# Recurrent mixer of a two-block network: when the chunk scores, the block transposes and the triangular solve stand in the program

## The chip, the cores and the metric

The kernel runs on one core of a Trainium2 chip. The metric is device time in microseconds (us) of one launch, from the core's clock. Before the change it is 1166.73 us, the median of 3 runs (1165.8 to 1170.56). Lower is better.

## The reference, cut to what matters

Two transformer blocks run on one sequence of 256 tokens and 1024 channels, all in float32. The change lies in the second layer of the first block, a recurrent time mix (WKV). Cut to what is touched:

```python
xr, xw, xk, xv, xa, xg = [h + xx * mu[i] for i in range(6)]   # xx: the token before, minus h
r, k, v = xr @ w_r, xk @ w_k, xv @ w_v
g = sigmoid(xg @ g1) @ g2
kk = heads(k * k_k); kk = kk / norm(kk)                        # 16 heads of 64
k = k * (1 + (a - 1) * k_a)
# per token t and head:
sa = state @ (-kk_t)
state = state * w_t + outer(sa, kk_t * a_t) + outer(v_t, k_t)
y_t = state @ r_t
y = groupnorm(y) * ln_w + ln_b + sum(r * k * r_k) * v
h = h + (y * g) @ w_o
```

## The kernel before, in words

The recurrence is not run token by token. The 256 tokens are cut into 4 chunks of 64. Within a chunk the dependence of each token's `sa` on the earlier tokens is a unit triangular system, and it is solved by blocks of 32 tokens. 16 heads x 4 chunks x 2 blocks give 128 systems of 32 x 32, one in each partition.

The function `rwkv` writes the stage in this order; the names are those that the profile prints for tiles.

- `k`: the keys' product in two halves (`key_half`), heads 0 to 7 and heads 8 to 15. Weights of `k`, `v` and `g` are used whole in float32, so each such product is two rows of the trace. While a half runs, `between0` or `between1` is called after each quarter.
- `keys(j)`, for a quarter j of the heads: VectorE and ScalarE build `AR` and `BK`, the scaled keys and queries. `squares(j)` multiplies the squares (`sqk`) with a pattern and gathers norms in `ssps`; `rkk(j)` forms the products for the bonus (`rk`).
- `scores(c, g)`: for chunk c and half g of the heads, 8 products on TensorE (`sce`, `sco`; 16 rows of the trace), then two masked copies on VectorE into `SC`.
- `norms()`: VectorE takes `ss` from `ssps`, and 16 small copies on SyncE's queue bring it into `pd`, one partition for each system. VectorE inverts `pd` to `ip`.
- `by_problems(g, bs)`: TensorE transposes the scores into `rb`, and copies bring them into `Ab`, one half of the tile `ABX`. The other half, `Xb`, starts with zeros and the inverses on its diagonal.
- `solve(s)`, s = 0 to 30: forward substitution on VectorE, small operations `tb<-ABX` and `ABX<-ABX,tb`, each waiting for the one before it.
- `values(0)`, `values(1)`: the product `v` in two halves, 8 steps of two instructions each, written as a generator (`next(v0)`, `next(v1)`), as are the gates (`g`, 4 steps). `by_tokens`: transposes of `BK` (`bkt`). `gate_turn`: transposes of the gate (`gt`, then `gz`, `gh`, `gl` on VectorE and ScalarE).
- Behind the solve: `xt` and `x` (X1) transpose its result, `q` and a second `x<-SC,X` form the block that couples the two halves of a chunk, `coefs` (`cf`) sums the bonus, `busy` are 8 products that fill time. Then `WY`, `U` and `S` run the chunks.

Weights come by DMA on SyncE's queue, 512 KB a chunk (`raw`), in the order in which the program takes them, into 4 buffers; where they are split, ScalarE makes `hi` and VectorE or GpSimd `lo`. PSUM has 8 banks (`bank`), shared by all of these.

The order of instructions on each engine is not exactly that of the code: the framework's scheduler orders them when the program is built, by the order written and by its own estimate of when operands and buffers are ready. Each engine then runs its own list in order. `L355`, `L358`, `L340`, `L343` and `L352` are the helpers `mm`, `tr`, `tt`, `stt` and `act`, so operations are told apart by their tiles.

Of the kernel before, what the change touches and what calls it, by code (L numbers as in the profile page):

```python
# [18 lines left out]
P = 128  # L19
T = 256  # L20
D = 1024
KD = 8
# [112 lines left out]
def full(name, layer, k, c0):  # L135
    return (name, layer, k * P, P, 0, ((c0, P),))
# [126 lines left out]
class Kern:  # L263
# [485 lines left out]
    def rwkv(self, sums, nxt):  # L749
        nc = self.nc  # L750
        h = self.h
        sp = self.sp
        ws = self.ws
# [39 lines left out]
        def mix(i, k, out):  # L793
            self.stt(out, xx[:, k, :], self.pv(f"mu{i}", k), hn[:, k, :], ALU.mult, ALU.add)
# [60 lines left out]
        for k in range(KD):  # L855
# [11 lines left out]
            if 3 <= k < 7:  # L867
                i, j = (k - 3) // 2, 2 * ((k - 3) % 2)
# [30 lines left out]
        def keys(j):  # L899

            ms, ps = two(j), psk[j]
            u, kku = self.mid("u", (P, 2, T)), self.mid("kku", (P, 2, T))
            for m in range(2):
                self.act(kku[:, m, :], half(ps, m), AF.Copy, scale=self.pv("k_k", 2 * j + m))
            for m in range(2):
                self.act(u[:, m, :], av(ms)[:, m, :], AF.Identity, scale=ka[:, 2 * j + m:2 * j + m + 1],
                         bias=ika[:, 2 * j + m:2 * j + m + 1])
            sq = self.mid("sqk", (P, 2, T))
            self.act(flat(sq), flat(kku), AF.Square)
            self.stt(arv(AR, j, 0), c4(kku), -1.0, dd(ms)[:, :, :, 0:64], ALU.mult, ALU.mult)  # L910
            t, kp = self.mid("t", (P, 2, T)), self.mid("kp", (P, 2, T))
            self.stt(t, av(ms), 1.0, kku, ALU.add, ALU.mult)
            self.tt(arv(BK, j, 0), c4(t), c4(di(ms)), ALU.mult)
            self.tt(flat(kp), ps, flat(u), ALU.mult)
            self.tt(arv(BK, j, 1), c4(kp), c4(di(ms)), ALU.mult)
            kps[j] = kp
            return sq

        def squares(j, sq):
            if not ssps:  # L920
                ssps.append(self.bank("ssps"))
            for m in range(2):
                mm = 2 * j + m
                self.mm(ssps[0][0:16, 0:T], self.cst("hind", 128)[:, mm * 16:(mm + 1) * 16], sq[:, m, :], mm == 0, mm == 7)
# [13 lines left out]
        def rkk(j):  # L938

            o = flat(rk[:, two(j), :])  # L940
            self.tt(o, o, flat(kps.pop(j)), ALU.mult)


        def key_half(g, between):
            pss = [self.bank("k") for _ in range(2)]
            for kk in range(4):
                w = ws.take_whole([full("rwkv_w_k", 0, k, m * P) for k in (2 * kk, 2 * kk + 1) for m in range(4 * g, 4 * g + 4)])
                for i, k in enumerate((2 * kk, 2 * kk + 1)):
                    for m in range(4):
                        self.mm(half(pss[m // 2], m), w[4 * i + m], xk[:, k, :], k == 0 and m % 2 == 0, k == KD - 1)  # L950
                between(kk)
            psk[2 * g], psk[2 * g + 1] = pss
# [5 lines left out]


        xv, xg = [self.xp.tile([P, KD, T], F32, tag=t, name=n) for t, n in (("xh", "xv"), ("xl", "xg"))]  # L960
        key_half(0, between0)
        sqs = {}

        def between1(kk):
            if kk < 2:
                sqs[kk] = keys(kk)
            else:
                squares(kk - 2, sqs[kk - 2])
                rkk(kk - 2)
            for k in (2 * kk, 2 * kk + 1):  # L970
                mix(5, k, xg[:, k, :])

        key_half(1, between1)


        psv = [[None, None] for _ in range(2)]

        def values(n):
            for tt in range(2):
                psv[tt][n] = self.bank("v")  # L980
            for k in range(KD):
                if k % 2 == 0:
                    ws.take_whole([full("rwkv_w_v", 0, q, (4 * n + i) * P) for q in (k, k + 1) for i in range(4)])
                    wt = ws.whole_chunk
                for tt in range(2):
                    self.mm(psv[tt][n], xv[:, k, tt * P:(tt + 1) * P], wt[:, 512 * (k % 2):512 * (k % 2) + 512], k == 0, k == KD - 1)
                yield


        SC = [pair("SC")[:, 0:4096].rearrange("p (i x t) -> p i x t", i=32, x=2) for _ in range(2)]  # L990
        tri = self.cst("tri", 128)
# [22 lines left out]
        def by_problems(g, bs):  # L1014
            for b in bs:
                p0 = 64 * b + 32 * g
                for e in range(2):
                    ps = self.bank("rb")
                    for i in range(16):
                        self.tr(ps[0:32, i * 32:(i + 1) * 32], SC[g][32 * b:32 * b + 32, :, 0, 32 * b + 16 * e + i],  # L1020
                                32, 32 * b)
                    o = Ab[p0:p0 + 32, 16 * e:16 * e + 16, :].rearrange("p a b -> p (a b)")
                    if e == 0:
                        nc.vector.tensor_copy(out=o, in_=ps[0:32, :])
                    else:
                        self.act(o, ps[0:32, :], AF.Copy)


        ip = self.tiny("ip", [P, 32], tag="pd")
        ABX = self.slot("ABX", (P, 2, 32, 32))  # L1030
        Ab, Xb = ABX[:, 0], ABX[:, 1]

        cf = self.tiny("cf", [P, 2, 16], tag="cf", bufs=3)
        cfps = []
# [16 lines left out]
        def solve(s):  # L1051
# [8 lines left out]
            for a, b in h:  # L1060
                o = Xb[:, s + 1 + a:s + 1 + b, 0:w]
                self.tt(o, o, tv[:, a:b, :], ALU.add)


        def gates():
            psg = self.bank("g")
            seg = [((0, P),), ((P, 32), (None, 96))]
            for k in range(KD):
                if k % 4 == 0:
                    ws.take_whole([("rwkv_g1", 0, q * P, P, 0, seg[i]) for q in range(k, k + 4) for i in range(2)])  # L1070
                    wt = ws.whole_chunk
                for tt in range(2):
                    self.mm(psg[:, tt * 160:tt * 160 + 160], xg[:, k, tt * P:(tt + 1) * P],
                            wt[:, 2 * P * (k % 4):2 * P * (k % 4) + 160], k == 0 and tt == 0, k == KD - 1)
                if k % 2:
                    yield psg

        v0, v1, ga = values(0), values(1), gates()
        next(v0)
        for j in (2, 3):  # L1080
            sqs[j] = keys(j)
        for _ in range(2):
            next(v0)
        for j in (2, 3):
            squares(j, sqs[j])
        norms()
        next(v0)
        for c in range(4):
            scores(c, 0)
            next(v0)  # L1090
        for c in range(4):
            scores(c, 1)
            psg = next(ga)
        next(v0, None)
        nc.vector.memset(Xb, 0.0)
        nc.vector.reciprocal(out=ip, in_=pd)
        nc.vector.tensor_copy(out=Xb.rearrange("p a b -> p (a b)")[:, 0:1024:33], in_=ip)
        for j in (2, 3):
            rkk(j)
        for g in range(2):  # L1100
            for b in range(2):
                by_problems(g, (b,))
        self.tt(Ab, Ab, ip.unsqueeze(2).to_broadcast([P, 32, 32]), ALU.mult)

        gm = self.mid("gm")
        gmt = gm[:, 0:448].rearrange("p (t c) -> p t c", t=2)
# [20 lines left out]
            q, o = slice(32, 64), slice(T, 2 * T)  # L1127
            self.tt(gh[q, o], z[q, o], gh[q, o].bitcast(F32), ALU.subtract)

        for s in range(14):  # L1130
            solve(s)
        for g in range(2):
            next(v1)
            by_tokens(g, (0, 1))
            next(v1)
            by_tokens(g, (2, 3))
        gate_turn()
        for s in range(14, 31):
            solve(s)
        for _ in range(4):  # L1140
            next(v1)
        self.dump("Xb", ABX)


# [12 lines left out]
        for b in range(2):  # L1157
            for e in range(4):
# [1 line left out]
                for i in range(8):  # L1160
                    self.tr(ps[0:32, i * 64:(i + 1) * 64], Xb[64 * b:64 * b + 64, 8 * e + i, :], 64, 64 * b)
                turned(lambda g: SC[g][32 * b:32 * b + 32, :, 0, 32 * b + 8 * e:32 * b + 8 * e + 8], ps)
        coefs(0)
        X1 = self.xp.tile([64, 2, 32, 32], F32, tag="xl", name="X1")
        for e in range(4):
            ps = self.bank("x1")
            for i in range(8):
                self.tr(ps[0:32, i * 64:(i + 1) * 64], Xb[0:64, :, 8 * e + i], 64, 0)
            turned(lambda g: X1[0:32, g, :, 8 * e:8 * e + 8], ps)
        coefs(1)  # L1170
        ms, mv = self.tiny("ms", [P, 2, 16], tag="cf", bufs=3), self.tiny("mv", [P, 4, 16], tag="mv", bufs=1)

        col = lambda g: SC[g][32:64, 0:4, 0, 40].rearrange("p (a b) -> p a b", a=2)
# [26 lines left out]
        for g in range(2):  # L1200
            for e in range(2):
                ps = self.bank("x21")
                for i in range(16):
                    ch = 16 * e + i
                    self.mm(ps[0:32, i * 32:(i + 1) * 32], X1[32:64, g, ch, :], SC[g][32:64, ch, 0, 32:64])
                if g == 0:
                    coefs(2 + e)
                o = SC[g][0:32, 16 * e:16 * e + 16, 0, 32:64]
                iv = ps[0:32, :].rearrange("p (a b) -> p a b", a=16)
                if e == 0:  # L1210
                    nc.vector.tensor_copy(out=o, in_=iv)
                else:
                    self.act(o, iv, AF.Copy)
# [68 lines left out]
        for c in range(4):  # L1282
# [4 lines left out]
            for g in range(2):  # L1287
# [9 lines left out]
                for e in range(2):  # L1297
                    q = slice(256 * e, 256 * e + 256)
# [14 lines left out]
            if c < 3:  # L1313
                for g in range(2):
# [6 lines left out]
                    for par in range(2):  # L1321
                        q = slice(64 * par, 64 * par + 64)
# [790 lines left out]
```

## Time and profile before

| | |
|---|---|
| median of 3 runs | 1166.73 us |
| profiled execution, its own time | 1166.81 us |
| its span (first to last instruction) | 1164.9 us |
| mean granted TensorE clock | 0.967 |
| TensorE (PE) busy | 1112.2 us, 95% |
| VectorE (DVE) busy | 859.5 us, 74% |
| ScalarE (ACT) busy | 575.7 us, 49% |
| DMA, mean share of 16 engines by the main queue | 51.7% |

The span and the 1.9 us around it make the profiled execution's time. Engine names in rows: PE is TensorE's matmul, PEld its weight load, DVE VectorE, ACT ScalarE, POOL GpSimd, SPq SyncE's DMA queue. A granted clock of 1.00 is 2.4 GHz, 0.50 is 1.2 GHz. An instruction's length on PE runs to its modelled end and overlaps with the next; where a rate is wanted, starts are compared.

### The profile page before, as it was taken

To read this page: it belongs to the slowest core of one execution; us is meant where nothing else is said; L and a number is where in the kernel's file an instruction comes from. 1 tells how busy PE (TensorE), PEld (TensorE's weight loads), DVE (VectorE), ACT (ScalarE), POOL (GpSimd) and SP (SyncE) were. 2 spreads that over 40 slices of the span, in tenths; PEclk is the share of its full clock that TensorE was granted. 3 is DMA by queue.
4 is the path that set the end of the run, shared out by engine and by line. 5 is a ranking of instruction groups with operands and counts; after the bars stand their busy time and mean duration, and the time that the engine had idled before them with its cause. 6 is when DMAs were issued, how large, how long until landed. Compare 5 with 4: busy or idle time off the path is not lost. (4 is left out here: it accounts for less than half of the span.)

```text
span 1164.9 us, 21766 instructions
## 1 busy us (share of the span) xinstructions
PE 1112.2 (95%) x8782; PEld 1036.7 (89%) x8782; DVE 859.5 (74%) x1563; ACT 575.7 (49%) x912; POOL 190.1 (16%) x138
## 2 busy tenths in 40 slices
PE   8799999999999899999999998899899997999997
PEld 7699999999867579899999998897798997999886
DVE  6879898557955935889876569799886958965444
ACT  5565444345631335664454546364454654755342
POOL 1310000010010030210000002776354014000000
PEclk9899999999999859999999999899899998999999
DMA  8459997653433300378865463534234552555552
GB/s 285 153 189 321 318 327 255 199 182 118 142 126 93 109 2 16 125 277 312 302 217 182 163 200 109 181 130 142 73 127 150 179 180 74 175 186 178 184 185 87
DMA packets 57814, 202.47 MB, mean 174 GB/s; under 512 B 6896, under 2 KB 8560, under 8 KB 57712
## 3 DMA queue, kind: packets, MB, share of 16 engines
q1 hardware_dynamic: 57712, 201.07, 51.7%
q8 instruction: 69, 1.13, 0.4%
q14 instruction: 33, 0.27, 0.1%
HBM read 199.98 MB, written 1.05 MB: 173 GB/s over the span
## 5 line engine op out<-in xcount | busy, mean ns | idle before, releaser
L185 ACT ACTIVATE hi<-raw 128x1024 fp32r<-128x1024 f32 (+1 forms) x310 | 323.3, 1048 | 269.2 <-PE ps L355 179.3
L186 DVE TENSOR_TENSOR lo<-raw,hi 128x1024 fp32r<-128x1024 f32 (+1 forms) x258 | 315.5, 1227 | 144.0 <-ACT hi L185 143.6
L355 PE MATMUL ps<-xh,hi 128*128 128x256 f32 x1104 | 316.6, 287 | 2.1 <-ACT hi L185 1.6
L355 PE MATMUL ps<-xl,hi 128*128 128x256 f32 x1104 | 314.3, 285 | 4.0 <-DVE xl L343 3.9
L355 PE MATMUL ps<-xh,lo 128*128 128x256 f32 x1104 | 312.0, 283 | 1.4 <-POOL lo L186 1.1
L355 PEld LDWEIGHTS ps<-xl,hi 128*128 128x128 f32 x1104 | 210.9, 191 | 5.3 <-DVE xl L343 4.8
L355 PEld LDWEIGHTS ps<-xh,hi 128*128 128x128 f32 x1104 | 210.1, 190 | 4.0 <-ACT hi L185 2.9
L355 PEld LDWEIGHTS ps<-xh,lo 128*128 128x128 f32 x1104 | 211.1, 191 | 2.3 <-POOL lo L186 1.3
L186 POOL TENSOR_TENSOR lo<-raw,hi 128x1024 fp32r<-128x1024 f32 x52 | 126.0, 2438 | 116.0 <-ACT hi L185 76.0
L343 DVE SCALAR_TENSOR_TENSOR cva<-up,cwh,cva 128x256 f32<-128x256 f32 x232 | 103.1, 481 | 3.2 <-ACT cva L352 1.1
L355 PE MATMUL ps<-zl,hi 128*128 128x256 f32 x352 | 99.6, 283 | 0.0
L355 PE MATMUL ps<-zh,lo 128*128 128x256 f32 x352 | 99.4, 283 | 0.0
L355 PE MATMUL ps<-zh,hi 128*128 128x256 f32 x352 | 98.7, 280 | 0.0
L254 POOL TENSOR_TENSOR sq<-sq 128x512 f32<-128x512 f32 x17 | 23.3, 1375 | 450.4 <-ACT sq L352 450.3
L343 DVE SCALAR_TENSOR_TENSOR ada<-ada,cb 128x1024 f32<-128x1024 f32 x48 | 58.6, 1221 | 12.2 <-DMA ada<-in_ada_dram 11.7
L355 PEld LDWEIGHTS ps<-zh,hi 128*128 128x128 f32 x352 | 66.9, 190 | 0.0
L355 PEld LDWEIGHTS ps<-zh,lo 128*128 128x128 f32 x352 | 66.1, 188 | 0.0
L355 PEld LDWEIGHTS ps<-zl,hi 128*128 128x128 f32 x352 | 65.8, 187 | 0.0
L355 PE MATMUL ps<-hi,zl 128*128 128x256 f32 (+1 forms) x160 | 56.1, 350 | 0.0
L355 PE MATMUL ps<-hi,zh 128*128 128x256 f32 (+1 forms) x160 | 56.0, 350 | 0.0
L355 PE MATMUL ps<-lo,zh 128*128 128x256 f32 (+1 forms) x160 | 55.9, 350 | 0.0
L352 ACT ACTIVATE s<-z 128x256 f32<-128x256 f32 x44 | 18.3, 416 | 59.4 <-DVE z L340 59.3
(439 smaller groups left out, 2286.8 us busy)
## 6 DMA issues: line engine op xcount, KB each, us to landing
raw<-in_w_dram SPq DMA_DIRECT2D x325, 512.0 KB
ada<-in_ada_dram SPq DMA_DIRECT2D x48, 512.0 KB
h<-in_x_dram SPq DMA_DIRECT2D x8, 128.0 KB
cb<-in_c_dram SPq DMA_DIRECT2D x2, 512.0 KB
out_dram<-ht SPq DMA_DIRECT2D x3, 256.0 KB
raw<-in_w_dram SPq DMA_DIRECT2D x2, 256.0 KB
cstt<-in_cst_dram SPq DMA_DIRECT2D x1, 448.5 KB
poolw<-in_poolw_dram SPq DMA_DIRECT2D x1, 256.0 KB
```

The source lines that it names most:

```text
L185: self.nc.scalar.activation(out=hi[:, s], in_=raw[:, s], func=AF.Copy)
L186: eng.tensor_tensor(out=lo[:, s], in0=raw[:, s], in1=hi[:, s].bitcast(F32), op=ALU.subtract)
L254: e.tensor_tensor(out=self.parts[0], in0=self.parts[0], in1=self.parts[-1], op=ALU.add)
L343: self.nc.vector.scalar_tensor_tensor(out=out, in0=a, scalar=s, in1=b, op0=op0, op1=op1, **k)
L352: self.nc.scalar.activation(out=out, in_=a, func=f, **k)
L355: self.nc.tensor.matmul(out=out, lhsT=lhsT, rhs=rhs, start=start, stop=stop, skip_group_check=True)
```

## The change

It moves work within `rwkv`; no operation is dropped.

- The scores of the first half of the heads move from between the values' steps into the keys' second half (`between1`), two chunks behind each of its last two quarters. The mixes for the gate (`xg`) move to the two quarters before.
- The block transposes of the first half (`by_problems(0, ...)`) move between the first steps of the values. Their four copies into `ABX` are all on ScalarE; of the second half's four, two stay on VectorE.
- The scores of the second half and the norms follow after three steps of the values, then the second half's transposes, and the whole solve is written in one piece, ahead of the gates' product, of `bkt`, of five of the first eight steps of the values and of all eight of the second.
- `coefs` moves from behind the solve to among the steps of `values(1)`, `gate_turn` from the middle of the solve to behind `xt`.
- `Xb` is zeroed by GpSimd instead of VectorE.

```diff
+        def between1(kk):
+            if kk < 2:
+                sqs[kk] = keys(kk)
+                for k in range(4 * kk, 4 * kk + 4):
+                    mix(5, k, xg[:, k, :])
+                return
+            squares(kk - 2, sqs[kk - 2])
+            rkk(kk - 2)
+            for c in (2 * kk - 4, 2 * kk - 3):
+                scores(c, 0)
...
-                    if e == 0:
+                    if e == 0 and g == 1:
                         nc.vector.tensor_copy(out=o, in_=ps[0:32, :])
                     else:
                         self.act(o, ps[0:32, :], AF.Copy)
...
+        nc.gpsimd.memset(Xb, 0.0)
+
         v0, v1, ga = values(0), values(1), gates()
         next(v0)
         for j in (2, 3):
             sqs[j] = keys(j)
-        for _ in range(2):
-            next(v0)
+        next(v0)
+        by_problems(0, (0,))
+        next(v0)
+        by_problems(0, (1,))
+        scores(0, 1)
         for j in (2, 3):
             squares(j, sqs[j])
+        scores(1, 1)
         norms()
-        next(v0)
-        for c in range(4):
-            scores(c, 0)
-            next(v0)
-        for c in range(4):
-            scores(c, 1)
-            psg = next(ga)
-        next(v0, None)
-        nc.vector.memset(Xb, 0.0)
+        scores(2, 1)
+        scores(3, 1)
+        for j in (2, 3):
+            rkk(j)
         nc.vector.reciprocal(out=ip, in_=pd)
...
-        for j in (2, 3):
-            rkk(j)
-        for g in range(2):
-            for b in range(2):
-                by_problems(g, (b,))
+        for b in range(2):
+            by_problems(1, (b,))
         self.tt(Ab, Ab, ip.unsqueeze(2).to_broadcast([P, 32, 32]), ALU.mult)
+        for s in range(31):
+            solve(s)
+        for _ in range(4):
+            psg = next(ga)
...
-        for s in range(14):
-            solve(s)
         for g in range(2):
+            for cs in ((0, 1), (2, 3)):
+                next(v0)
+                by_tokens(g, cs)
+        next(v0)
+        for i in range(8):
             next(v1)
-            by_tokens(g, (0, 1))
-            next(v1)
-            by_tokens(g, (2, 3))
-        gate_turn()
-        for s in range(14, 31):
-            solve(s)
-        for _ in range(4):
-            next(v1)
+            if i % 2:
+                coefs(i // 2)
...
-        coefs(0)
+        gate_turn()
...
-        coefs(1)
...
-                if g == 0:
-                    coefs(2 + e)
```

What stands on TensorE around the block transposes. Before, all 128 follow the last step of the gates' product (`g`):

```order
L355 MATMUL sco<-AR,BK 128x128
L355 MATMUL g<-raw,xg 128x160 x4
L358 MATMUL rb<-cstt,SC 32x32 x128
L355 MATMUL v<-raw,xv 128x512 x2
L358 MATMUL bkt<-cstt,BK 128x128 x8
```

After the change, the first half's stand between steps of the values, ahead of the second half's scores:

```order
L355 MATMUL v<-raw,xv 128x512 x4
L358 MATMUL rb<-cstt,SC 32x32 x32
L355 MATMUL v<-raw,xv 128x512 x2
L358 MATMUL rb<-cstt,SC 32x32 x32
L355 MATMUL sce<-AR,BK 128x128
```

and the second half's stand behind those scores, with the gates' product, `bkt` and the values behind them:

```order
L355 MATMUL v<-raw,xv 128x512 x2
L358 MATMUL rb<-cstt,SC 32x32 x64
L355 MATMUL g<-raw,xg 128x160 x16
L358 MATMUL bkt<-cstt,BK 128x128 x8
L355 MATMUL v<-raw,xv 128x512 x2
L358 MATMUL bkt<-cstt,BK 128x128 x8
```

One block of 128 transposes has become three of 32, 32 and 64, and 4 + 2 + 2 instructions of `v` are ahead of the last of them, where 16 of `v` and 16 of `g` were.

What stands on TensorE around `xt`, the first product that needs the solve. Before:

```order
L358 MATMUL gt<-cstt,gm 96x128
L355 MATMUL v<-raw,xv 128x512 x8
L358 MATMUL xt<-cstt,ABX 32x64 x64
L355 MATMUL cf<-rk,cstt 16x256 x2
L358 MATMUL x_4524<-cstt,ABX 32x64 x8
```

After the change:

```order
L355 MATMUL v<-raw,xv 128x512 x4
L355 MATMUL cf<-rk,cstt 16x256 x2
L358 MATMUL cf<-cstt,cft 128x16 x2
L358 MATMUL xt<-cstt,ABX 32x64 x64
L358 MATMUL gt<-cstt,gm 128x128
L358 MATMUL gt<-cstt,gm 96x128
```

The bonus sums `cf` have moved from behind `xt` to ahead of it, `gt` the other way.

The end of the solve on VectorE, with what is among it (`lo` is the split of the gate's second weights, `SC<-xt` empties the banks of `xt`). Before:

```order
L340 TENSOR_TENSOR tb<-ABX 128x87
L186 TENSOR_TENSOR lo<-raw,hi 128x1024
L340 TENSOR_TENSOR ABX<-ABX,tb 128x3x29
L186 TENSOR_TENSOR lo<-raw,hi 128x1024
L340 TENSOR_TENSOR tb<-ABX 128x60
L1153 COPY SC<-xt 32x32x8
L340 TENSOR_TENSOR ABX<-ABX,tb 128x2x30
L1153 COPY SC<-xt 32x32x8
```

After the change:

```order
L340 TENSOR_TENSOR tb<-ABX 128x87
L340 TENSOR_TENSOR ABX<-ABX,tb 128x3x29
L340 TENSOR_TENSOR tb<-ABX 128x60
L340 TENSOR_TENSOR ABX<-ABX,tb 128x2x30
L340 TENSOR_TENSOR tb<-ABX 128x31
L340 TENSOR_TENSOR ABX<-ABX,tb 128x31
L186 TENSOR_TENSOR lo<-raw,hi 128x1024 x2
L1154 COPY SC<-xt 32x32x8 x6
```

The two splits stand behind the last step of the solve now, and still ahead of all copies of `xt`.

## Rows read from the trace of the kernel before

**Rows 1.** The page, part 1 (busy, share, instructions) and part 2 (granted clock, tenths).

```profile
PE 1112.2 (95%) x8782; PEld 1036.7 (89%) x8782; DVE 859.5 (74%) x1563; ACT 575.7 (49%) x912; POOL 190.1 (16%) x138
...
PEclk9899999999999859999999999899899998999999
```

**Rows 2.** Table by stretch: length, busy per engine (instructions), granted clock, DMA, GB/s.

```profile
350.00:371.00 21.00, 21.00 (x175) 14.40 (x172) 10.75 (x18) 0.26 (x1) 0.00 (x0) 1.00 0.34 103
371.00:375.00 4.00, 4.00 (x114) 4.00 (x112) 2.14 (x4) 3.58 (x8) 0.00 (x0) 0.93 0.43 135
375.00:381.00 6.00, 6.00 (x27) 3.73 (x25) 4.97 (x21) 1.18 (x2) 0.00 (x0) 0.50 0.00 0
...
396.00:404.00 8.00, 3.20 (x33) 1.97 (x33) 8.00 (x35) 0.37 (x1) 1.98 (x2) 0.86 0.37 121
...
415.00:419.00 4.00, 4.00 (x99) 3.22 (x98) 0.88 (x2) 2.96 (x7) 3.30 (x3) 0.93 0.02 4
419.00:433.00 14.00, 13.54 (x176) 10.22 (x174) 3.89 (x7) 1.74 (x4) 1.16 (x1) 0.50 0.01 2
```

**Rows 3.** TensorE's timeline up to the solve's end: start, length, instruction, count.

```profile
345.37 1.90 PE L355 MATMUL ssps<-sqk,cstt 128*16 128x256 f32 x8
347.20 1.98 PE L355 MATMUL v<-raw,xv 128*128 128x512 f32 x4
...
350.20 1.99 PE L355 MATMUL v<-raw,xv 128*128 128x512 f32 x4
...
370.64 5.08 PE L358 MATMUL rb<-cstt,SC 32*32 32x32 f32 x128
375.65 3.78 PE L355 MATMUL v<-raw,xv 128*128 128x512 f32 x4
379.22 1.91 PE L358 MATMUL bkt<-cstt,BK 128*128 128x128 f32 x8
...
382.80 1.04 PE L358 MATMUL bkt<-cstt,BK 128*128 128x128 f32 x8
```

**Rows 4.** SyncE's queue, first of 16 copies of the squared norms.

```profile
347.81 2.12 SPq L935 DMA_DIRECT2D pd<-ss  x3
```

**Rows 5.** VectorE's timeline from the norms to the last step [idle before <- releaser].

```profile
360.48 0.35 DVE L1096 RECIPROCAL ip<-pd 128x32 f32<-128x32 f32 x1 [2.88 <-DMA pd<-ss]
...
376.37 1.23 DVE L340 TENSOR_TENSOR ABX<-ABX,ip 128x1024 f32<-128x1024 f32 x1 [0.79 <-ACT ABX L352]
...
389.49 0.75 DVE L349 TENSOR_SCALAR gz<-gt 128x256 f32<-128x256 f32 x2 [1.67 <-PE gt L358]
...
400.19 1.21 DVE L186 TENSOR_TENSOR lo<-raw,hi 128x1024 fp32r<-128x1024 f32 x1
...
404.55 0.17 DVE L340 TENSOR_TENSOR ABX<-ABX,tb 128x31 f32<-128x31 f32 x1
```

**Rows 6.** ScalarE's timeline, split of the second gate weight chunk.

```profile
391.71 1.06 ACT L185 ACTIVATE hi<-raw 128x1024 fp32r<-128x1024 f32 x1 [1.02 <-DMA raw<-in_w_dram]
```

**Rows 7.** TensorE's timeline, two pieces of the tail behind the solve.

```profile
396.25 1.73 PE L358 MATMUL xt<-cstt,ABX 64*32 64x64 f32 x25
...
419.62 1.91 PE L355 MATMUL q<-X,SC 32*32 32x32 f32 x32
```

**Rows 8.** Groups of TensorE, 396 to 433.2 us: busy us, mean ns, idle before.

```profile
L355 PE MATMUL cf<-rk,cstt 128*16 128x256 f32 x16 | 7.7, 614 | 0.0
L355 PE MATMUL x<-SC,X 32*32 32x32 f32 x128 | 7.2, 236 | 0.0
L358 PE MATMUL xt<-cstt,ABX 64*32 64x64 f32 x64 | 6.5, 265 | 4.8 <-DVE ABX L340 4.8
L355 PE MATMUL q<-X,SC 32*32 32x32 f32 x128 | 5.1, 203 | 0.0
L358 PE MATMUL x<-cstt,ABX 64*32 64x64 f32 x32 | 3.8, 306 | 0.0
...
L358 PE MATMUL cf<-cstt,cft 16*128 16x16 f32 x2 | 0.4, 273 | 0.5 <-ACT cft L352 0.5
```

More of the change, by code (lines that the diff above doesn't have):

```diff
@@ L960, in rwkv @@
         xv, xg = [self.xp.tile([P, KD, T], F32, tag=t, name=n) for t, n in (("xh", "xv"), ("xl", "xg"))]
[L961 to L987, printed above, removed]
         SC = [pair("SC")[:, 0:4096].rearrange("p (i x t) -> p i x t", i=32, x=2) for _ in range(2)]
@@ L1029, in rwkv @@
         ip = self.tiny("ip", [P, 32], tag="pd")
-        ABX = self.slot("ABX", (P, 2, 32, 32))
-        Ab, Xb = ABX[:, 0], ABX[:, 1]
         cf = self.tiny("cf", [P, 2, 16], tag="cf", bufs=3)
@@ L1062, in solve, with values @@
                 self.tt(o, o, tv[:, a:b, :], ALU.add)
+        key_half(0, between0)
+        sqs = {}
+        def between1(kk):
[8 more added lines that the diff above has]
+                scores(c, 0)
+        key_half(1, between1)
+        psv = [[None, None] for _ in range(2)]
+        def values(n):
+            for tt in range(2):
+                psv[tt][n] = self.bank("v")
+            for k in range(KD):
+                if k % 2 == 0:
+                    ws.take_whole([full("rwkv_w_v", 0, q, (4 * n + i) * P) for q in (k, k + 1) for i in range(4)])
+                    wt = ws.whole_chunk
+                for tt in range(2):
+                    self.mm(psv[tt][n], xv[:, k, tt * P:(tt + 1) * P], wt[:, 512 * (k % 2):512 * (k % 2) + 512], k == 0, k == KD - 1)
+                yield
         def gates():
@@ L1076, in gates @@
                     yield psg
+        ABX = self.slot("ABX", (P, 2, 32, 32))
+        Ab, Xb = ABX[:, 0], ABX[:, 1]
+        nc.gpsimd.memset(Xb, 0.0)
         v0, v1, ga = values(0), values(1), gates()
```

## The prediction

> **What bounds the kernel now.** The page comes first. TensorE is busy 95% of the span, and the row of its granted clock has one dip, an 8 and a 5 in the fourteenth and fifteenth slice [rows 1]. So the kernel runs as long as TensorE's list does, and the recurrent mixer is where that list runs badly. The table by stretch tells how [rows 2]. From 350 to 371 us TensorE is busy 21.00 of 21.00 at 1.00. It is still busy throughout (4.00 of 4.00) when the clock falls, within 371 to 375 (0.93), and 375 to 381 is all at 0.50. From 396 to 404 it is busy only 3.20 of 8.00. Then the clock is 0.50 again, up for a moment at 415 to 419 (0.93), and 0.50 for 419 to 433.
>
> The timelines say who is waited for. TensorE's 128 block transposes `rb` start at 370.64, behind all scores and gate products, and the clock falls within them [rows 2, 3]. On VectorE the product of `ABX` with `ip` starts at 376.37 and the last step of the solve at 404.55 [rows 5]. `xt`, the next thing that TensorE can do once its values are used up, stood idle 4.8 us for `ABX` [rows 8]. So the solve ends last there, and what stands behind it is small work at the low clock.
>
> **The change, part by part.** The operations are the same ones; what counts is what TensorE no longer waits for, and at which clock it does the rest. The order decides whether the solve still ends last, so that comes first.
>
> *Start of the solve.* VectorE's chain begins at `ssps`. In TensorE's list its second half (the eight rows at 345.37 [rows 3]) stands behind three steps of `v`, before and after, but after the change also behind five scores and 64 of the `rb`. A step of `v` and a score take 3.00 us together (347.20 to 350.20), of which the step is 1.98 with the overlap at its end: 1.1 for a score [rows 3]. An `rb` is 5.08/128 = 0.04. So `ssps` moves back by 5 x 1.1 + 64 x 0.04 = 8.0 us. The 16 copies, which started at 347.81 [rows 4], and `ip`, which waited for them until 360.48 [rows 5], move along: `ip` at 368.5. With 0.35 for it, 0.2 for the diagonal's copy (an estimate, from the last step's 0.17, as small a tile) and 1.23 for the product, the solve starts at 370.3, against 376.37 + 1.23 = 377.6. The second half's transposes are done by then: TensorE has three more scores, a step of `v` and 64 `rb` behind `ssps`, 3.3 + 2.0 + 2.5 = 7.8 us, against 12.7 for the copies.
>
> *End of the solve.* It took 27.1 us (377.6 to 404.7), with a wait of 1.67 and 0.75 of work for the gate and two splits `lo` of 1.21 in it [rows 5]. The gate and the splits leave it: 22.3, so it ends at 392.6. The splits stand behind it and ahead of the copies of `xt`: VectorE is free for those at 395.0.
>
> *When TensorE comes to `xt`.* Before, at 396.25 [rows 7]. Three terms move this.
> - The `rb` come in pieces of 32, 32 and 64 with products between. I take it that the clock then holds. Four rows of `v` at the low clock took 3.78 against 1.98, and eight of `bkt` 1.91 against 1.04 [rows 3]: 1.80 + 0.87 = **2.7 us less**. If each of the three pieces made the clock fall once, that would be two falls more than now: the term lies between -2.7 and +5.4, and I take the end that the stretch at 1.00 before the first `rb` is nearer to, in which small and large products alternate.
> - `cf` comes ahead of it. Its 16 rows took 7.7 us in the tail, and its two transposes 0.4 with a wait of 0.5 [rows 8]. At full clock eight rows of the same shape (`ssps`, 128*16 128x256) take 1.90 [rows 3], so 3.8 here and 0.9 for the transposes: 4.7 more ahead, 8.6 less behind, **3.9 us less**.
> - `gt` leaves, half of what eight `bkt` take (1.04), and comes back behind `xt`: nothing.
>
> That gives 396.25 - 2.7 + 4.7 - 0.5 = 397.7, and VectorE is ready at 395.0. TensorE no longer waits for the solve; the cover is 2.7 us thick, and each us beyond costs one. `xt` took 6.5 us and 4.8 of waiting [rows 8]; at the rate of its first 25 (1.73 [rows 7]) 64 take 4.4: **6.9 us less**.
>
> *The tail.* `x`, `q`, `x<-SC,X` come in the same order. `cf` is gone from between, and this has a price. The stretch of 415 to 419 at 0.93 [rows 2] lies among the `cf`, and in it 96 of the 128 `q` ran in 5.1 - 1.91 = 3.2 us, while the other 32 took 1.91 at 0.50 [rows 7, 8]. Without it I put all `q` at the low clock: 3 x 1.91 - 3.2 = **2.5 us more**. `q` also waits for VectorE's copy of the last `x`, which `cf` covered. No row shows that wait bare: from 0.5 (`cf` for its copy [rows 8]) to 1.67 (`gz` for its transposes [rows 5]); I take **0.8 us more**, near the first, which is also TensorE waiting for one copy.
>
> Where the clock falls in the tail no row can tell for the new order. I let it fall in `xt` or `x`: all small tiles here did so, `rb` with TensorE busy 4.00 of 4.00 and the clock at 0.93, then 0.50 [rows 2]. The Trainium skill, "TensorE: Matmul & The Clock Gate", section "Part 4: PE-mode transpose", says that transposes don't count as busy for the clock as products do; by that the clock falls too, and the trace agrees at `rb`. The same page, section "HAM oscillation — how this bites in real kernels", puts the low clock down to idle gaps of TensorE; by that the tail would keep 2.4 GHz and the time would be rival A's. The trace disagrees: at `rb` there was no gap.
>
> *At nothing.* Scores of the first half inside the keys delay the second half's keys by two scores, 2.2 us; VectorE, which builds them, is free half the time (10.75 of 21.00 busy [rows 2]), and six instructions of `v` and 64 `rb` stand between them and the first score that needs them. If that cover is gone, it costs at most the 2.2. Two copies change to ScalarE, which has 0.26 of 21.00 to do there [rows 2]. The zeros of `Xb` go to GpSimd, idle there (0.00), and are wanted only with `ip`. On SyncE's queue one weight load stood behind three of the norms' copies and now stands behind fourteen, some 14 x 2.12/3 = 10 us behind the first [rows 4] instead of 2; the values that want it stand behind the gates' product and three pairs of `bkt` and `v`, each 1.04 + 1.98 [rows 3], so it has about 9 us to land in, and what is missing of that would cost as much.
>
> *Sum:* -2.7 - 3.9 - 6.9 + 2.5 + 0.8 = **-10.2 us**. On the profiled execution, 1166.81 (span 1164.9 and 1.9 around it), that is 1156.6; the median before is 0.08 lower, which changes nothing. Everything behind `WY` follows TensorE and moves with it.
>
> **The rivals.**
> - *A, the clock holds through the tail.* For: no idle gap ahead of `xt` any more. Against: `rb` and the end of `q` fell with TensorE busy. Then `x` takes 32 x 1.73/25 = 2.2 instead of 3.8, `q` 128/96 x 3.2 = 4.3 instead of 7.6, `x<-SC,X` half of 7.2: 1.6 + 3.3 + 3.6 = 8.5 less, 1148.1.
> - *B, the solve still ends last.* A late norm copy, or the second gate chunk, whose split waits for a load as it did before (1.02 at 391.71 [rows 6]) and now stands ahead of all copies of `xt` on VectorE. Decides from 2.7 us on. With 6.9 of the gain gone: 1166.8 - 3.3 = 1163.5.
> - *C, slower: the clock falls at the first `rb` and stays low until the gates' product is done.* Scores, squares, three pieces of `rb` are then a stretch like 350 to 371, 21 us [rows 2]. By 5.69/3.02 for `v` and `bkt` together [rows 3], work at 0.50 takes 1.88 times as long: 18.5 more, 1175.1. It eats the whole gain from 11.6 us of such work on. Against: scores and values in turn held 1.00 there.
>
> **How the numbers follow.** The forecast has 58 in 100, with its own range of 1152 to 1160; A 20, its partial forms included, B 15, C 7. The range 1146 to 1163.5 reaches over A and to B's time, and leaves out C and the far ends. About 0.5%, 5.8 us, is what can be told from no change here: faster is below 1160.9, slower above 1172.6. The forecast, A and two of B's 15 are faster, 80; the rest of B and one of C same, 14; slower 6.
>
> **What would show it.** Right: TensorE busy without a gap from 335 us to `xt`; clock 1.00 where `rb` and `bkt` now stand; the last `ABX` of the solve before 394 and `xt` near 398; the clock at 0.50 from within `xt` or `x` to the first `WY`, which starts near 423 instead of 433. Wrong: idle of TensorE ahead of `xt` with `ABX` or `SC` as releaser (B); a clock under 1.00 between 348 and 372 (C); `q` at 1.00 (A).

## The result and the profile after

The kernel after took 1155.11 us (median; 1153.52 to 1157.15), the kernel before 1167.16 beside it: ratio 0.9893, 95% interval 0.9867 to 0.992. Run anew with the experiments it gave 1155.4 and 0.9891 (0.9875 to 0.9906). That is 12 us faster, about 1%, and both intervals lie below 1; 1156.6 was forecast, 1146 to 1163.5 the range.

The profiled execution of after took 1153.52, its span 1151.7. On its page the granted clock's 8 and 5 in the fourteenth and fifteenth slice [rows 1] are now a 9 and a 7, and TensorE is busy 10.8 us less:

```profile
PE 1101.4 (96%) x8782; PEld 1032.8 (90%) x8782; DVE 856.1 (74%) x1560; ACT 574.9 (50%) x914; POOL 190.9 (17%) x139
...
PEclk9899999999999979899999999899999999999999
```

The table by stretch of after answers to [rows 2] (length, busy per engine with instructions, granted clock, DMA, GB/s):

```profile
350.00:371.00 21.00, 20.93 (x241) 16.17 (x239) 9.39 (x16) 5.59 (x11) 0.00 (x0) 1.00 0.21 59
371.00:375.00 4.00, 4.00 (x23) 2.70 (x22) 3.27 (x11) 2.50 (x6) 0.00 (x0) 1.00 0.60 223
375.00:381.00 6.00, 6.00 (x21) 3.09 (x20) 6.00 (x37) 1.73 (x4) 0.00 (x0) 1.00 0.40 112
396.00:404.00 8.00, 7.00 (x95) 5.36 (x94) 4.92 (x14) 4.61 (x14) 1.92 (x2) 1.00 0.72 260
404.00:408.00 4.00, 2.25 (x59) 2.11 (x58) 3.65 (x9) 3.30 (x10) 0.00 (x0) 1.00 0.00 0
408.00:419.00 11.00, 11.00 (x185) 10.15 (x182) 4.83 (x8) 4.99 (x11) 7.48 (x4) 0.50 0.02 4
419.00:425.00 6.00, 6.00 (x80) 5.94 (x79) 1.10 (x2) 0.96 (x2) 1.89 (x2) 0.50 0.01 3
```

1.00 stands where 0.93 and 0.50 stood (371 to 381), 396 to 404 is busy 7.00 of 8.00 instead of 3.20, and one stretch at 0.50 is left, from 408 us.

To measure the stage itself, take the two ends on TensorE that both kernels share: the first `ssps`, up to which the list is the same, and the first `WY` behind the tail. In before (start, length, instruction, count):

```profile
334.43 1.04 PE L355 MATMUL ssps<-sqk,cstt 128*16 128x256 f32 x4
...
433.17 3.05 PE L355 MATMUL WY<-UV,SC 128*64 128x64 f32 x28
```

and in after, with the rows between that answer to [rows 3, 7, 8] (in brackets the idle time ahead and its releaser):

```profile
336.18 1.04 PE L355 MATMUL ssps<-sqk,cstt 128*16 128x256 f32 x4
...
361.81 2.54 PE L358 MATMUL rb<-cstt,SC 32*32 32x32 f32 x64
...
396.43 1.04 PE L355 MATMUL cf<-rk,cstt 128*16 128x256 f32 x4
397.93 0.29 PE L358 MATMUL cf<-cstt,cft 16*128 16x16 f32 x2 [0.46 <-ACT cft L352]
398.15 3.54 PE L358 MATMUL xt<-cstt,ABX 64*32 64x64 f32 x64
401.62 0.66 PE L358 MATMUL gt<-cstt,gm 128*128 128x128 f32 x4
402.21 1.08 PE L358 MATMUL x<-cstt,ABX 64*32 64x64 f32 x16
403.83 1.08 PE L358 MATMUL x<-cstt,ABX 64*32 64x64 f32 x16 [0.54 <-ACT SC L352]
406.65 6.01 PE L355 MATMUL q<-X,SC 32*32 32x32 f32 x128 [1.75 <-ACT X L352]
...
414.41 7.03 PE L355 MATMUL x<-SC,X 32*32 32x32 f32 x128
421.37 3.67 PE L355 MATMUL WY<-UV,SC 128*64 128x64 f32 x32
```

So the stage took 433.17 - 334.43 = 98.74 us before and 85.19 after, 13.55 less. The rest of the spans' 13.2 lies outside: the stage began 1.75 later in this execution, and the part behind `WY` was 1.4 shorter (the second profile of after began it 0.5 later than before, and was 2.6 longer behind `WY`; such amounts come and go).

VectorE's timeline of after answers to [rows 5]:

```profile
371.03 0.35 DVE L1099 RECIPROCAL ip<-pd 128x32 f32<-128x32 f32 x1 [6.58 <-DMA pd<-ss]
...
371.93 1.22 DVE L340 TENSOR_TENSOR ABX<-ABX,ip 128x1024 f32<-128x1024 f32 x1
...
393.57 0.19 DVE L340 TENSOR_TENSOR ABX<-ABX,tb 128x31 f32<-128x31 f32 x1
393.68 2.35 DVE L186 TENSOR_TENSOR lo<-raw,hi 128x1024 fp32r<-128x1024 f32 x2
398.81 2.53 DVE L1154 COPY SC<-xt 32x256 f32<-32x256 f32 x6 [2.78 <-PE xt L358]
...
403.17 0.75 DVE L349 TENSOR_SCALAR gz<-gt 128x256 f32<-128x256 f32 x2
403.84 0.73 DVE L1154 COPY X<-x 32x256 f32<-32x256 f32 x2
404.86 0.43 DVE L340 TENSOR_TENSOR gl<-gz,gh 128x256 fp32r<-128x256 f32 x1 [0.29 <-ACT gh L352]
```

The solve ends 11 us sooner than in before, 12.7 counted from the first `ssps`, and now VectorE waits for TensorE's `xt` (2.78), not the other way round.

### The profile page after: what moved, and what is told of

Its sections match the earlier page's. It is cut to its first block, busy times and chain, and to the rows that moved or that the text cites. A ratio compares the mean times of both kernels' runs of the same rounds, so it can differ in the third digit from the quotient of the medians.

```text
span 1151.7 us, 21771 instructions
## 1 busy us (share of the span) xinstructions
PE 1101.4 (96%) x8782; PEld 1032.8 (90%) x8782; DVE 856.1 (74%) x1560; ACT 574.9 (50%) x914; POOL 190.9 (17%) x139
```

## The experiments

All ratios are to the kernel before; "after" without more is 1155.1 to 1155.4 by its two medians. "The stage" is the time from the first `ssps` to the first `WY` in the profiled execution: 98.74 us before, 85.19 and 86.02 in the two profiles of after. Clock falls are read from the granted clock in stretches of 1 us.

**One part alone: cf ahead of xt, the rest as before.**

```diff
-        for _ in range(4):
+        for i in range(4):
             next(v1)
+            coefs(i)
...
-        coefs(0)
...
-        coefs(1)
...
-                if g == 0:
-                    coefs(2 + e)
```

> The kernel before with one part of the change alone: the eight products cf (and their two transposes) stand between the last values, ahead of xt; everything else is in the old order, so the solve starts late as before. Theory (the solve ends last before; cf only fills TensorE's wait for it): VectorE's last step of the solve stays at 404 to 405 us, TensorE reaches xt about 5 us later than before and its wait there shrinks from 4.8 us to nearly nothing; cf's 8.6 us leave the tail, q loses its short stretch at full clock (+2.5) and waits bare for the copy of x (+0.8 to +1.75). Net 4 to 6 us faster than before, about 1161 to 1163, under half of the change's 12. Rival (placing cf is the larger part, since its work at the low clock was what cost): 8 us or more faster, 1159 or less. Rival (cf was free cover behind xt, and moving it gives nothing): within 1.5 us of before.

1162.03 us, 0.9955 (0.9942 to 0.9969): 5.3 us faster. Its chain of waits on TensorE, 396 to 428 us (us in total, times, longest), shows what became of the 4.8 us of [rows 8]:

```profile
PE xt L358 <- DVE ABX L340: 0.6, 1, 0.6
PE q L355 <- ACT X L352: 0.6, 1, 0.6
```

TensorE came to `xt` at 402.86, 5.05 us later counted from the first `ssps` (335.99 here); the solve's last step, at 405.94, came no sooner than before (404.38, so counted; 404.55 there):

```profile
402.86 1.85 PE L358 MATMUL xt<-cstt,ABX 64*32 64x64 f32 x30
405.94 0.17 DVE L340 TENSOR_TENSOR ABX<-ABX,tb 128x31 f32<-128x31 f32 x1
```

The first theory holds: under half of the gain, and got by filling the wait.

**The other part alone: solve early, cf back among x and q.**

```diff
-            if i % 2:
-                coefs(i // 2)
...
+        coefs(0)
         X1 = self.xp.tile([64, 2, 32, 32], F32, tag="xl", name="X1")
...
+        coefs(1)
...
+                if g == 0:
+                    coefs(2 + e)
```

> The kernel after with cf alone put back among x, q, as before the change; solve early as in the change. Theory (the prediction's sum): cf back behind xt costs what its move was put at, 3.9 us, less the 2.5 and 0.8 that its absence cost q, so about 1 us slower than after; TensorE reaches xt about 4.7 us sooner (393.5 us) and would then wait for VectorE, which is ready at 396.0: 2 to 3 us of waiting come back, so 3 to 4 us slower than after in all, 1158 to 1159. Rival (cf keeps TensorE in larger products in the tail, and the clock stays at 1.00 through q): the clock falls later than 408 us or not at all before x<-SC,X, q's bare wait of 1.75 us is covered, and the kernel is 2 to 5 us faster than after, 1150 to 1153.

1156.44 us, 0.9909 (0.9888 to 0.993): 10.9 faster than before, 1 us from after and not told from it. Either part takes most of the idle time, so 5.3 and 10.9 don't add up to more than 12. Both theories' sizes were off. TensorE came to `xt` at 392.62, when VectorE was still at `lo` (until 393.95), and yet:

```profile
PE x L358 <- ACT X L352: 1.0, 1, 1.0
PE xt L358 <- ACT SC L352: 0.2, 1, 0.2
```

The cover is thicker than the distance of those two ends: the first 32 rows of `xt`, eight to a bank of PSUM, ran before TensorE waited for a copy. And this profile has something that the first of after had not, behind the third piece of `rb`, in a list that is the same up to there (table by stretch, then the row of `g`, which took 4.61 in after):

```profile
362.00:366.00 4.00, 4.00 (x25) 3.96 (x23) 0.46 (x1) 0.58 (x1) 0.00 (x0) 0.57 0.03 6
362.30 6.29 PE L355 MATMUL g<-raw,xg 128*128 128x160 f32 x32
```

Even so its stage took 84.73 us, no longer than in after. In this tail 14 of the 16 rows of `cf` ran at full clock, about 0.24 us each by their starts, since the clock fell only at 406.8. So once the solve is early, neither the medians (1 us, not told from none) nor the stage show a gain from having `cf` ahead of `xt`.

**All rb in one block.**

```diff
-        by_problems(0, (0,))
         next(v0)
-        by_problems(0, (1,))
...
-        for b in range(2):
-            by_problems(1, (b,))
+        for g in range(2):
+            for b in range(2):
+                by_problems(g, (b,))
```

> The kernel after with its 128 block transposes rb in one block again, behind the scores of the second half; nothing else is moved. Theory (the prediction's clock term): the granted clock falls below 1.00 within or just behind the block, as it did at 371 to 381 us before, and the products behind it lose about 2.7 us; the copies to pd still land later than rb ends, so the solve is not delayed, and TensorE comes to xt 2.7 us later with more cover: 2 to 3.5 us slower than after, about 1158. Rival (the order of rb has no part in the clock; the fall of before had to do with what stood around it): 1.00 throughout, the same time as after within 0.5 us.

1158.12 us, 0.9924 (0.9904 to 0.9944), about 3 us slower than after, at the edge of what the intervals tell. The clock fell within the block, to 0.50 from 360.3 to 363.7:

```profile
360.00:364.00 4.00, 4.00 (x34) 3.91 (x32) 0.68 (x1) 0.93 (x2) 0.00 (x0) 0.57 0.04 6
```

So the clock falls in a block of them with TensorE busy 4.00 of 4.00, in all three profiles that have the block (before, `cf` ahead of `xt`, and this one). But pieces are no guarantee: of seven profiles with a third piece of 64 rows, three fall behind it (`g` then takes 6.29 us instead of 4.61). What the block costs is open: the medians say 3 us, but in the profiled execution, which at 1155.99 was 2 us under its median, TensorE came to `xt` only 0.5 us later than in after, counted from the first `ssps` (62.49 against 61.97).

**Solve late by four operations.**

```diff
+        for _ in range(4):
+            self.tt(Ab, Ab, Ab, ALU.max)
         for s in range(31):
             solve(s)
```

> The kernel after with four more VectorE operations of about 1.22 us each ahead of the solve (the maximum of Ab with itself, which changes no value): the solve starts and ends 4.9 us later. Theory (TensorE reaches xt at 398.15, VectorE is ready at 396.0, so the cover is 2.1 us): TensorE waits 2.5 to 3 us for SC at xt, and the kernel is about 2.8 us slower than after, 1158. Rival (the solve still ends last somewhere that the wait at xt does not show): the full 4.9 us, 1160. Rival (other slack takes it up, for instance the copies of xt, which VectorE makes one after another): under 1 us.

1161.1 us, 0.9949 (0.9928 to 0.9969): 5.9 slower than after. The wait is the size that was expected, but it is not the whole price, and the time is nearer to the first rival's. TensorE's timeline (this execution took 1157.0):

```profile
396.90 1.85 PE L358 MATMUL xt<-cstt,ABX 64*32 64x64 f32 x30
400.63 0.23 PE L358 MATMUL xt<-cstt,ABX 64*32 64x64 f32 x1 [1.89 <-DVE ABX L340]
401.08 0.23 PE L358 MATMUL xt<-cstt,ABX 64*32 64x64 f32 x1 [0.22 <-DVE ABX L340]
401.81 3.35 PE L358 MATMUL xt<-cstt,ABX 64*32 64x64 f32 x32 [0.50 <-ACT SC L352]
405.09 1.12 PE L358 MATMUL gt<-cstt,gm 128*128 128x128 f32 x4
406.14 3.59 PE L358 MATMUL x<-cstt,ABX 64*32 64x64 f32 x32
410.33 7.00 PE L355 MATMUL q<-X,SC 32*32 32x32 f32 x128 [0.60 <-ACT X L352]
```

2.6 us of waiting at `xt`, and the clock fell at 402.1, in the two profiles of after at 408.1 and 405.7: 3.6 to 4.7 us sooner, counted from the first `ssps` (334.92 here). The fall came 5.2 us behind the start of `xt`; five profiles with the solve early and the same list through `x` have it 7.6 to 10.2 us behind, so this one lies outside what those five show. Half of `xt`, `gt`, `x` and all of `q` (7.00) then stood at the low clock. The stage took 91.12, which is 5.9 and 5.1 more than in the profiles of after. Little of that is waiting: `x` no longer waits 0.54 and `q` waits 0.60 instead of 1.75, so the 2.6 are 0.9 net. The other 4 to 5 us are nearly all the low clock.

**After once more, and the wait ahead of q filled.**

> The kernel after, unchanged, run anew beside the next three and profiled once more. In its first profile the granted clock held 1.00 through the three pieces of rb; the kernel with cf put back, whose list is the same up to there, fell to 0.50 at 362.7 us behind the third piece. Theory (the split of rb keeps the clock): 1.00 from 340 to 400 us again. Rival (whether the clock falls at the third piece changes from run to run, and the split only makes it rarer or shorter): a stretch at 0.50 of 3 to 4 us behind the third piece in this run, g at 6.3 us instead of 4.6. Either way the median is within 1.5 us of 1155.1, and xt to WY is as in the first profile: the clock falls within q, q takes 5.5 to 6.5 us.

Measured 1155.4 (above). No stretch at the third piece; the clock fell at 405.7, 0.3 us into `q`, which took 6.81:

```profile
405.41 6.81 PE L355 MATMUL q<-X,SC 32*32 32x32 f32 x128 [1.75 <-ACT X L352]
```

What was expected of the repeat held, but for `q`, 0.3 us above its bound.

```diff
+        self.busy(8)
         for g in range(2):
             for e in range(2):
                 ps = self.bank("q")
```

> The kernel after with eight more of the idle products busy (128x256, bf16) ahead of q, in the 1.75 us in which TensorE waits for the copy of X; their result is not used. They take 8 x 0.118 = 0.95 us at full clock. Theory (the clock falls in q because of the idle time ahead of it): the fall comes later than 408 us, within or behind the second half of q; q nearer 4.3 us than 6.0; 1 to 3 us faster than after. Rival (it falls because of q itself, small products with TensorE busy throughout): the fall at 408 to 409 as before, the time as after within 0.5 us.

1154.94 us (1149.62 to 1156.47), 0.9877 (0.9857 to 0.9896), not told from after. In its profile the clock fell later, at 410.7, and all of `q` ran at 1.00:

```profile
405.32 1.03 PE L355 MATMUL busy<-cstt 128*128 128x256 bf16 x8 [0.68 <-ACT X L352]
406.39 4.21 PE L355 MATMUL q<-X,SC 32*32 32x32 f32 x128
410.52 1.76 PE L355 MATMUL busy<-cstt 128*128 128x256 bf16 x8
```

Between 405.32 and the fall, 5.4 us, there is no gap. So filling the wait puts the fall off (12.8 us behind the start of `xt`, against 7.6 to 10.2), and small products make the clock fall without a gap all the same. Whether the idle time less or the large products more put it off, this run can't say. From the start of `xt` to the first `WY` it took 21.30 us, against 23.22 and 24.03 in after. Of these 1.9 and 2.7 us the execution lost 1.7 elsewhere, behind the third piece of `rb`, where this profile has a fall.

**Large products all along the tail.** The edit above, and:

```diff
-                if (g, e) == (1, 1):
-                    self.busy(8)
+                self.busy(8 if (g, e) == (1, 1) else 4)
...
                     self.mm(ps[0:32, i * 32:(i + 1) * 32], X1[32:64, g, ch, :], SC[g][32:64, ch, 0, 32:64])
+                self.busy(4)
```

> The kernel after with 36 more of the idle products busy: eight ahead of q, four behind each of the first three groups of q, four behind each of the four groups of x<-SC,X. At full clock they take 36 x 0.118 = 4.2 us, 0.95 of it in the wait ahead of q. Theory (large products between the small ones hold the clock at 1.00 up to WY): q 4.3, x<-SC,X 3.6, WY 1.9 us, 8 us less against 3.3 more, 4 to 5 us faster than after. Rival (the small products pull the clock down all the same): 28 of them at 0.236 are 6.6 us more, 1161 to 1162.

1150.58 us (1149.73 to 1153.06), 0.9851 (0.9835 to 0.9867): 4.8 faster than after beside it. The clock held, and the median is the first theory's:

```profile
408.00:420.00 12.00, 11.94 (x255) 9.91 (x252) 6.21 (x10) 5.67 (x13) 7.48 (x4) 1.00 0.01 3
420.00:424.00 4.00, 4.00 (x75) 3.73 (x73) 0.83 (x2) 1.18 (x3) 1.89 (x2) 1.00 0.02 4
```

Its terms are not all the theory's. From the start of `xt` to the end of `WY` this execution took 24.30 us, against 26.69 and 27.50 in after, 2.4 and 3.2 less: by their starts `x<-SC,X` took 4.5 instead of 3.6 and the 36 products 4.9 instead of 4.2. This execution took 1153.06, over its median, and has a fall behind the third piece of `rb` (1.7); what is left of the 4.8 stands in the medians of four runs each and in no row.

**Turning of the gate ahead of xt** (`gate_turn()` from behind `xt` to behind the last `coefs`).

> The kernel after with the turning of the gate ahead of xt instead of behind it. Theory (q's bare wait of 1.75 us, which the prediction put at 0.8, comes from gz, gl and gh, which stand ahead of the copies of X on VectorE and ScalarE): the wait shrinks to 0.5 to 0.8 us, about 1 us faster than after. Rival (the wait is the copy itself behind the last x, with its latency): 1.5 us or more remain, no gain. Against both: gl and gh may fall among the copies of SC, and xt waits 0.5 to 1 us instead.

1154.13 us (1150.74 to 1161.74), 0.9886 (0.9859 to 0.9913), not told from after. What it trades is in its waits:

```profile
PE q L355 <- DVE X L1155: 0.9, 1, 0.9
PE xt L358 <- ACT SC L352: 0.6, 1, 0.6
```

1.75 became 0.9, so `gz`, `gl` and `gh` were about half of `q`'s wait; 0.6 comes back at `xt`, in place of 0.54 at `x`. The stage took 83.83, which is 1.4 and 2.2 less than in the profiles of after; the medians don't tell it.

**The third piece of rb cut in two.**

```diff
             by_problems(1, (b,))
+            if b == 0:
+                next(ga)
...
-        for _ in range(4):
+        for _ in range(3):
             psg = next(ga)
```

> The kernel after with the third piece of rb (64 rows in the trace) cut in two by the first eight rows of the gates' product g. Of the seven profiles with the piece whole, three show a stretch at 0.50 behind it (362 to 367 us), in which g took 6.29 us instead of 4.61. Theory (how many of these transposes stand in one piece decides): 1.00 from 340 us to q, nothing gained on the first profile of after, 1.7 us on those with the stretch; median 0 to 1.7 us below after's 1155.4, too little to be told by the ratio alone. Rival (the stretch comes whatever the pieces, at the end of a run of small work): a stretch below 1.00 between 360 and 368 us in this profile too.

1155.06 us, 0.9901 (0.9876 to 0.9926), not told from after. 1.00 there in this profile and in the three that follow with the cut; against three falls in seven without it that speaks for the theory and is no proof.

**Combinations.**

> Three edits on the kernel after together: the 36 more idle products busy (ahead of, between and behind the groups of q and x<-SC,X), the turning of the gate ahead of xt, and the third piece of rb cut in two. Theory (they are independent: the first gave 1155.4 to 1150.6, the second took 0.84 us of q's wait and cost 0.60 at xt, the third is worth 0 to 1.7): 1148.5 to 1150, clock at 1.00 from 340 us to behind WY. Rival (the wait ahead of q is now filled by busy products anyway, so that the turning only adds its 0.6 at xt): 1150.5 to 1151.5.

> As the kernel with the three edits, with half as many idle products: four ahead of q, two behind each of the first three groups of q, four (instead of eight) behind the last, two behind each group of x<-SC,X. Theory (half of them still hold the clock): 22 fewer products at 0.12 to 0.15 us each, 2.5 to 3 us faster than with all of them, 1146 to 1147. Rival (the clock is held by how much large work stands between the small): it falls to 0.50 within q or x<-SC,X, the tail takes 4 to 6 us more, 1151 to 1154.

All three edits: 1153.88 us, 0.99 (0.9866 to 0.9935), above what either theory said, and in two groups: five runs at 1150.53 to 1154.06 with a mean clock of 0.981 to 0.984, two at 1162 to 1163 with 0.971. With half the idle products the rival came true for the clock, down at 406.2 within `q`, and its time (1151 to 1154) was exceeded too: 1157.94 us, 0.9914 (0.9895 to 0.9934):

```profile
408.00:420.00 12.00, 11.88 (x168) 9.42 (x167) 3.85 (x6) 3.38 (x7) 5.94 (x4) 0.50 0.01 2
```

To see where the two groups come from, the idle products and the cut of `rb` without the turning of the gate:

> The kernel with the 36 more idle products busy and the third piece of rb cut in two, the turning of the gate left behind xt as in after. With the turning ahead of xt, five of seven runs took 1150.5 to 1154.1 us at a mean clock of 0.981 to 0.984 and two 1162 to 1163 at 0.971. Theory (36 products are just enough, and whether the clock holds through the tail changes from run to run): most runs at 1149 to 1152 us, now and then one near 1161; median 1150 to 1151. Rival (the turning ahead of xt, with its wait of 0.60 us there, let the clock fall in those two): all runs at 1148 to 1152. Rival (the cut rb moves the tail to where the clock falls): median above 1153.

1159.55 us (1151.65 to 1163.1), 0.9915 (0.989 to 0.9939). By the mean clocks one run held it (1151.65, mean clock 0.984), one in part (1154.94, 0.978), four did not (1158.88 to 1163.1, 0.970 to 0.974). The profiled one is of these, with 1.00 up to 404 and then:

```profile
404.00:408.00 4.00, 3.32 (x39) 2.61 (x39) 3.38 (x7) 3.28 (x10) 0.72 (x1) 0.61 0.00 0
408.00:420.00 12.00, 11.94 (x149) 9.23 (x147) 3.25 (x5) 3.59 (x8) 6.76 (x4) 0.50 0.01 3
```

It fell at 404.9, at the end of `x`, as the first idle products began, and these, now at 0.50, didn't bring it back until 432. So the turning of the gate is not needed for the long runs. The median is above 1153, as the last rival has it; but whether that is the cut, which moves the tail in time, the chip (these runs were on another one than those of the two kernels above) or chance from run to run, 6 runs can't say. So 1150.6 is, by the median of the four runs with the idle products alone, what the tail gives when the clock holds; with the cut of `rb` beside them it doesn't hold in every run.

## Why the prediction was right

The way of the gain was the one forecast: the solve's first step comes early (373.2, which is 371.4 counted from the first `ssps` of before; 370.3 forecast), it ends early (393.8, so counted 392.0; 392.6 forecast), TensorE comes to `xt` at 396.4, so counted (397.7 forecast), and no longer waits for the solve, and the low clock at 371 to 381 is gone. Rivals B and C didn't occur. The forecast was 10.2 us for a stage that gave 13.55 (12.7 in the second profile of after: 420.93 - 334.91 = 86.02). By its own terms:

- *The start of the solve.* `ssps` moved back by 7.9 us in the stage, 8.0 forecast, and it is still the copies that `ip` waits for (6.58). They took 13.5 us to it instead of 12.7. The weight load stands behind fourteen of them, as foreseen, and so ahead of the last two, as SyncE's queue in after shows (start, length; answers to [rows 4]):

```profile
357.50 9.47 SPq L935 DMA_DIRECT2D pd<-ss  x14
367.07 0.38 SPq L160 DMA_DIRECT2D raw<-in_w_dram  x1
367.50 1.31 SPq L935 DMA_DIRECT2D pd<-ss  x2
```

That a load among them costs the 0.8 is not shown by itself, but it fits: with all `rb` in one block no load stood among the sixteen, and they took 12.2 us to `ip`.

- *Clock term, 2.7.* Right in kind for after, too small: 6.00 us at 0.50 and 4.00 at 0.93 [rows 2] lose 3.0 + 0.3. Only `v` and `bkt` had been counted, not the end of `rb`. And the split is no switch: three falls in seven profiles, 1.7 us each. The block as one costs about 3 us by the medians and 0.5 up to `xt` in its one profile, so this term's size stays open.
- *cf, 3.9 less.* Four times 0.97 and 0.7 for its transposes ahead, as worked out. With the 2.5 and 0.8 that its absence was to cost `q`, the move was put at 0.6 net. Putting it back cost 1 by the medians (not told from none) and nothing in the stage (84.73). The 7.7 of before came from the low clock, and with the solve early `cf` behind `xt` runs at 1.00 for 14 of its 16 rows; so the 3.9 is not shown as a gain of this move. The part alone on before was worth 5.3, because there it fills a wait.
- *xt, 6.9 less.* No wait, and 3.47 us to `gt` instead of 4.4. The rate had been taken from the length of a row [rows 7], which runs to its last modelled end and holds a wait ahead of the 25th; by their starts the first 24 run 0.056 us apart in before and after alike. `gt` takes 0.59 behind it and is gone from ahead of it, so nothing, as put.
- *The cover of 2.7 us and "each us beyond costs one".* This step failed, on both sides. With `cf` behind, the cover was gone by the timeline and only 0.2 us of waiting came; with the solve 5 us late, 2.6 us of waiting at `xt` (0.9 net) went with 5.9 of time, since the clock fell about 4 us sooner.
- *The tail.* The clock was to fall within `xt` or `x`; in after it fell in `q` (408.1 and 405.7). So `x` ran at 1.00, 2.7 us with a wait of 0.54 in it instead of 3.8, and `q` took 6.0 to 6.8 instead of 7.6: a part of rival A. `q`'s bare wait was 1.75, not 0.8; the gate's operations had been left out, which stand ahead of and among the copies of `X` on both engines and are about half of it, as the turning ahead of `xt` shows.

What is 3.35 us better than forecast in the stage is mostly the clock in `x` and `q` (1.1 and 1.6), `xt` (0.9) and the clock term (0.6), less `q`'s wait (0.95): 3.25. That this nearly closes says little, since rows overlap by some tenths each and `xt` was reached 1.3 us sooner than forecast, of which only the 0.6 is explained.

Of the two rules weighed, neither came out whole. The Trainium skill, "TensorE: Matmul & The Clock Gate", section "HAM oscillation — how this bites in real kernels", puts the low clock down to idle gaps of TensorE. Here gaps count, but not alone: with the late solve a wait of 1.9 us brought the fall forward, but in the `rb` block the clock fell with TensorE busy 4.00 of 4.00, and with the wait ahead of `q` filled it fell after 5.4 us without a gap. The same page of the Trainium skill, section "Part 4: PE-mode transpose", says that transposes don't count as busy for the clock as products do. The transposes `xt`, `gt` and `x` ran here at 1.00 from 398.15 to 404.9, and the clock fell only behind them. So the prediction's "all small tiles here did so" was too strict.

## What to carry to other kernels

When TensorE waits for a chain on another engine, start the chain at the first moment its inputs allow and put whatever doesn't need it between: here the early start alone took 10.9 of the 12 us and filling the wait alone 5.3, since both remove the same wait. Price a wait by the clock that follows it as well: here 2.6 us of idle time ahead of small products (0.9 net) came with 4 to 5 us of low clock. And a stretch of small products can bring a cost of its own (`q` 7.00 us at 0.50 against 4.21 at 1.00). In the profiles here 36 large products put between them held the clock where it had not fallen before they began, and did not raise it where it had; 14 did not hold it.

## What was not expected of the hardware

- Products whose result nobody uses made the kernel faster: 36 of 128x256 (some 4.9 us by their starts) gave 4.8 net by the medians where the clock held; with 14 more it fell within `q`, and behind a clock already at 0.50 all 36 left it there for 27 us (404.9 to 432.2).
- The same list of instructions held the clock in one execution and lost it in the next, at the third piece of `rb`. Runs of the kernel with the idle products and the cut of `rb` are 7 to 11 us apart (1151.65 with a mean clock of 0.984, 1158.88 to 1163.1 with 0.970 to 0.974); the one of them that is profiled, at 1163.1, lost the clock at the end of `x`.
